# The output projection of a hybrid decoder layer: 648 tokens as block products in two passes over K, the other 384 tokens last

## The chip, the cores and the metric

The kernel runs on one core of a Trainium2 chip. The metric is the device time of one execution in microseconds (us), as the median of several runs. The core's engines work side by side: TensorE multiplies matrices (PE in the profile; PEld are its weight loads), VectorE (DVE) and ScalarE (ACT) do element-wise work, GpSimd (POOL) and SyncE (SP) mostly issue transfers between the core's memory and the chip's DRAM. ACT and POOL issue transfers too. Matmul results land in PSUM, and DVE or ACT must read them out before the bank is used again.

## The reference

One layer for a prompt of 1024 tokens and 8 sample tokens, 1032 tokens in all, in float32. Two branches, a retention and a diagonal state space model (S5), are gated and merged, and the merged rows go through one last projection and a norm:

```
merged = sigmoid(ga) * (ya @ w_pa) + sigmoid(gb) * (yb @ w_pb)     # 1032 x 2048
out = merged @ w_out                                              # w_out: 2048 x 2048
y = x + out * rsqrt(mean(out * out, -1) + EPS) * g_post
```

Only this projection and its norm are changed.

## The kernel before

**Precision.** Each float32 operand is split into a high part (what the matmul's input type holds, made by an ACT copy) and a low part (the rest, made by a DVE subtraction). A product is three matmuls into the same PSUM bank: high by high, high by low, low by high. So every weight tile of 128x512 costs ACT one cast (`whi`) and DVE one subtraction (`wlo`) before TensorE can use it. There are three buffers for each of the two.

**Block products.** All projections ahead of the last one are done by steps (`steps`, line 814). A step makes a 2x2 block of the result with seven products in place of eight, in the manner of Strassen: two output tiles of 128 features (`21` is the second) by two halves of the 1032 tokens, 516 tokens each, with the K dimension (the one that is summed over) also cut in two. The right sides of the seven products are sums and differences of blocks (`FORMS`: u1, t2, v1, t3, t1, t4, v2), made once per projection; the left sides are sums of weight tiles (`s1` to `s4`), made on DVE in each step by `prep`, two products ahead of their use. One product (`product`) is 4 k tiles x 3 matmuls x 2 halves of 258 columns, 24 matmuls. The evacuation after each product (`evac_p`) combines it with the products before it, on DVE, or copies it, on ACT. Products 2, 3, 5 and 6 of a step add into a PSUM tile that an earlier product of the step began, so that TensorE must wait there until the earlier one has been read: a product n+2 cannot start before the evacuation of n.

**The forms of a projection** are staged by `transition`: 28 tiles are loaded through eight buffers (`stg`, issued on POOL's queue) and split, two per product at its height, while the projection before still runs. The program orders work by product number: `at(g, f)` puts f behind product g, `slot()` lets one generator of background work do one piece after each product, and what is issued in order on an engine's queue also runs in order.

**Merge (w_pb, steps SB to SB+7).** `gated` multiplies by the gate. From the third step on, before adds the other branch with a DVE addition from a preloaded tile (`pp`), and writes the merged rows to DRAM (`mg_d`). TensorE's last product of it is followed by the output projection.

**Output projection, before**, is not in block products. (1) `out_rows`: the last 392 tokens stand on the columns; for each of 16 output tiles, 16 k tiles x 3 matmuls of 392 columns (lines 210 to 212, called by `linear`), 768 matmuls. The squares for the norm are made on ACT and added on POOL; the rows are finished in the background. (2) `out_tokens(0, 3, ...)`: the first 640 tokens in chunks of 128 stand as the stationary side, the weights move: 4 groups of 512 features x 16 k tiles x 3 chunks x 3 matmuls of 512 columns (line 1692), 576 matmuls. (3) `out_tokens(3, 2, True)`: the same for the last two chunks, 384 matmuls. In (2) and (3) one weight tile is split anew per k tile and group. In the last group of (3) each chunk is finished as soon as its last matmul is done: square and sum on ACT, product with g_post on DVE, a power on POOL, then four DVE instructions of 512 columns (line 1642), each with its store.

Of the kernel before, what the change touches and what calls it, by code (L numbers as in the profile page):

```python
# [18 lines left out]
D = 2048  # L19
# [8 lines left out]
TA = 640  # L28
SW = TOK - TA
THIRDS = [(0, 384), (384, 768), (768, TOK), (TA, TOK)]  # L30
# [48 lines left out]
def emit(ctx, tc, I, O):  # L79
# [65 lines left out]
    yb_d = dram("yb_d", [8, 128, TOK])  # L145
    mg_d = dram("mg_d", [16, 128, TOK])
# [667 lines left out]
    steps = [(kh, p) for kh in range(2) for p in range(NP)] + [(kh, p) for kh, n in (("glu", 4), ("pa", 8), ("pb", 8)) for p in range(n)]  # L814
    lim = [7 * len(steps)]
    qtile = {}

    def qslot(kh, n, i):
        j = (2 * n + i // 2 + {0: 0, 1: -2, "glu": -4, "pa": -6, "pb": -8}[kh]) % 16
# [7 lines left out]
    def stage(pool, kh, n, i, eng=P):  # L827
        r = stq[kh, n, i] = pool.tile([128, HT], F32, name="stg")
        if kh in (0, 1):
# [13 lines left out]
    def fetch(s):  # L843
# [3 lines left out]
        wd, m, q = (w_in, pairs[p][1], 2 * kh) if kh in (0, 1) else (I["w_" + kh], 2 * p, 0)  # L847
# [33 lines left out]
    def product(g):  # L881
# [7 lines left out]
        for i in range(4):  # L889
            xh, xl = qslot(kh, n, i)  # L890
            for a, b in ((wh, xh), (wh, xl), (wl, xh)):
                for j in range(2):
                    anchor["p"] = T.matmul(ps[:, j, 0:258], a[:, i, :], b[:, 258 * j:258 * j + 258],  # L893
                                           start=first and i == 0 and a is wh and b is xh,
                                           stop=n in (2, 5, 6) and i == 3 and a is wl, skip_group_check=True).ins
        return ps[:, :, 0:258]
# [499 lines left out]
    last_t = {}  # L1396

    def load_z(s, name):
# [4 lines left out]
        if kind == "pb" and p > 1 and (p < 7 or c):  # L1403
            zq[name, "p"] = ppp.tile([128, HT], F32, name="pp")
            A.dma_start(zq[name, "p"], pap_d[2 * p + r, :, HT * c:HT * c + HT])

    def gated(g, name, t, ps=None):
# [19 lines left out]
        elif (name, "p") in zq:  # L1427
            add(t, t, zq.pop((name, "p")), V)
            if c and p > 5:
                last_t[m] = t  # L1430
            P.dma_start(mg_d[m, :, cols], t)
        else:
            P.dma_start(t, pap_d[m, :, cols], accum_op=ALU.add)
            at(g + LAG, lambda: P.dma_start(mg_d[m, :, cols], t))
# [28 lines left out]
    mg, mgr = [None] * KD, {}  # L1463

    def mg_open(m):
        a = act.tile([128, 2, TOK], F32R, name=f"a{(6 + m) % 16}")
        mg[m] = a[:, 0, :], a[:, 1, :]

    def mg_load(m):
        mgr[m] = mgp.tile([128, SW], F32, name="mga")  # L1470
        A.dma_start(mgr[m], mg_d[m, :, TA:TOK])

    def mg_split(m, src=None):
        mg_open(m)
        split((mg[m][0][:, TA:TOK], mg[m][1][:, TA:TOK]), mgr.pop(m) if src is None else src)

    SE = len(steps) - 1
# [41 lines left out]
    for g in sorted(due):  # L1519
        late_work(g)  # L1520
# [273 lines left out]
```

## Time and profile before

| | |
|---|---|
| median of 3 runs (lowest to highest) | 2599.7 us (2599.66 to 2600.05) |
| profiled execution: its time | 2599.76 us |
| profiled execution: span of the trace | 2598.0 us |
| TensorE busy, of the span | 2579.8 us (99%) |
| DVE, ACT, POOL busy | 1900.0 (73%), 968.1 (37%), 686.9 us (26%) |
| mean granted TensorE clock | 0.999 |
| first matmul of the output projection | 2221.76 us |
| its part (2) begins, last matmul begins | 2360.53, 2587.58 us |

The span runs from the first to the last instruction; the execution's own time is 1.8 us longer. A row of a timeline shows start, duration, engine, line, operation, the tile written and the tiles read, and the form; in brackets the idle time of the engine before it and what ended that. Matmuls overlap, so that the pace of a row of matmuls is read from their starts, not from their durations.

### The profile page before, as it was taken

What the parts mean: (1) busy time and instruction counts of PE and PEld (TensorE: products, weight loads), DVE (VectorE), ACT (ScalarE), POOL (GpSimd) and SP (SyncE); (2) the same over time, 40 slices, a digit from 0 to 9 for tenths busy, and PEclk for the clock granted to TensorE, in tenths of its full rate; (3) what the DMA queues carried; (4) which work ended last, traced back from release to release, by engine and by line L of the source; (5) the groups of instructions that cost most, each with busy time, mean ns of one, the idle gap of its engine ahead of it and who ended that gap; (6) DMA issues with size and microseconds to landing.
All of it is one profiled execution on the core that took longest, in us unless ns stands there. A gap on an engine that the chain in (4) does not pass through costs nothing.

```text
span 2598.0 us, 51727 instructions
## 1 busy us (share of the span) xinstructions
PE 2579.8 (99%) x19748; PEld 2517.0 (97%) x19748; DVE 1900.0 (73%) x3949; ACT 968.1 (37%) x1707; POOL 686.9 (26%) x1140
## 2 busy tenths in 40 slices
PE   9999999999999999999999999999999999999998
PEld 8999999999999999999999999999999999998876
DVE  7655988898898877558976766677787878545555
ACT  6113233233233334343334444435542422443344
POOL 0103312222222222332334434334222221111011
PEclk9999999999999999999999999999999999999999
DMA  5886534434444437887788888888787786755667
GB/s 193 263 261 218 152 116 121 138 117 127 134 119 134 127 117 251 205 214 190 199 207 230 226 223 218 212 217 257 254 288 256 235 225 211 232 165 180 184 199 234
DMA packets 234072, 509.79 MB, mean 196 GB/s; under 512 B 32753, under 2 KB 55233, under 8 KB 233697
## 3 DMA queue, kind: packets, MB, share of 16 engines
q0 software_dynamic: 92496, 271.74, 37.4%
q1 hardware_dynamic: 103072, 177.46, 22.6%
q10 hardware_dynamic: 38256, 57.30, 7.3%
q8 instruction: 155, 2.54, 0.4%
q14 instruction: 93, 0.75, 0.1%
HBM read 343.74 MB, written 162.64 MB: 195 GB/s over the span
## 4 chain that ended last, share of the span: by engine, by line
PE 96%; DVE 2%; issue 1%; DMA 1%; ACT 1%; DVEq 0%; POOLq 0%; POOL 0%; ACTq 0%; SPq 0%
PE acc L893 68%; PE acc L1692 9%; PE mm L212 2%; PE mm L210 2%; PE mm L211 2%; PE acc L210 2%; PE acc L211 2%; PE acc L212 2%; PE misc L635 1%; PE misc L713 1%; PE misc L712 1%; PE misc L1097 1%; PE misc L1107 1%; PE misc L1076 1%; PE misc L663 1%
## 5 line engine op out<-in xcount | busy, mean ns | idle before, releaser
L893 PE MATMUL acc<-a,whi 128*128 128x258 f32 x10080 | 1635.2, 284 | 1.0 <-ACT whi L874 0.6
L893 PEld LDWEIGHTS acc<-a,whi 128*128 128x128 f32 x10080 | 1387.9, 190 | 5.5 <-issue 2.4
L893 PE MATMUL acc<-a,wlo 128*128 128x258 f32 x5040 | 1014.3, 282 | 0.0
L893 PEld LDWEIGHTS acc<-a,wlo 128*128 128x128 f32 x5040 | 779.5, 189 | 0.0
L84 DVE TENSOR_TENSOR wlo<-wraw,whi 128x512 fp32r<-128x512 f32 x496 | 340.1, 686 | 259.6 <-ACT whi L203 141.2
L874 ACT CAST whi<-wraw 128x512 fp32r<-128x512 f32 x360 | 223.5, 621 | 638.2 <-PE acc L893 473.3
L874 ACT CAST whi<-wr 128x512 fp32r<-128x512 f32 x270 | 167.4, 620 | 531.3 <-PE acc L893 459.8
L84 DVE TENSOR_TENSOR wlo<-wr,whi 128x512 fp32r<-128x512 f32 x270 | 184.6, 684 | 42.3 <-ACT whi L874 41.2
L1692 PE MATMUL acc<-whi,a 128*128 128x512 f32 x640 | 201.9, 396 | 0.0
L203 ACT CAST whi<-wraw 128x512 fp32r<-128x512 f32 x136 | 84.1, 620 | 203.8 <-PE acc L1692 69.0
L210 PE MATMUL mm<-a,whi 128*128 128x384 f32 (+1 forms) x448 | 145.0, 325 | 4.9 <-ACT whi L203 4.8
L1692 PEld LDWEIGHTS acc<-whi,a 128*128 128x128 f32 x640 | 120.2, 188 | 30.2 <-DVE z L84 2.1
L211 PE MATMUL mm<-a,whi 128*128 128x384 f32 (+1 forms) x448 | 145.1, 324 | 0.2 <-DVE a L364 0.2
L212 PE MATMUL mm<-a,wlo 128*128 128x384 f32 (+1 forms) x448 | 144.7, 323 | 0.1
L1692 PE MATMUL acc<-wlo,a 128*128 128x512 f32 x320 | 127.0, 397 | 0.0
L84 DVE TENSOR_TENSOR wraw<-wr 128x512 f32<-128x512 f32 x180 | 123.4, 685 | 2.5
L84 DVE TENSOR_TENSOR wlo<-wx,whi 128x512 fp32r<-128x512 f32 x78 | 53.8, 691 | 71.9 <-ACT whi L203 71.7
L84 DVE TENSOR_TENSOR u<-acc,p 128x516 f32<-128x516 f32 x90 | 62.2, 691 | 57.8 <-PE acc L893 55.8
L84 DVE TENSOR_TENSOR u<-acc,u 128x516 f32<-128x516 f32 x90 | 62.3, 693 | 54.6 <-PE acc L893 53.8
L84 DVE TENSOR_TENSOR p<-acc,p 128x516 f32<-128x516 f32 x90 | 62.3, 692 | 50.3 <-PE acc L893 50.2
L84 DVE TENSOR_TENSOR a<-stg,a 128x516 fp32r<-128x516 f32 x140 | 91.7, 689 | 7.0 <-DMA stg<-fm_d 4.0
L203 ACT CAST whi<-wx 128x512 fp32r<-128x512 f32 x78 | 48.4, 620 | 123.6 <-PE acc L1692 45.0
(373 smaller groups left out, 3496.2 us busy)
## 6 DMA issues: line engine op xcount, KB each, us to landing
wr<-in_w_in SPq DMA_DIRECT2D x280, 256.0 KB
pt_d<-u POOLq DMA_DIRECT2D x70, 258.0 KB, 3.3
u<-pt_d POOLq DMA_DIRECT2D x70, 258.0 KB, 5.0
wraw<-in_w_outB SPq DMA_DIRECT2D x65, 256.0 KB
wx<-in_w_outB SPq DMA_DIRECT2D x45, 256.0 KB
stg<-fm_d POOLq DMA_DIRECT2D x44, 258.0 KB, 4.5
wraw<-in_w_out SPq DMA_DIRECT2D x39, 256.0 KB
pt_d<-st POOLq DMA_DIRECT2D x35, 258.0 KB, 3.4
```

What stands on the lines that cost most here:

```text
L84: return (eng or V).tensor_tensor(out, a, b, op)
L203: anchor["a"] = A.copy(hi, raw).ins
L210: T.matmul(ps, wh[:, i, :], xh[:, t0:t1], start=first, stop=False)
L211: T.matmul(ps, wh[:, i, :], xl[:, t0:t1], start=False, stop=False)
L212: anchor["p"] = T.matmul(ps, wl[:, i, :], xh[:, t0:t1], start=False, stop=last).ins
L635: T.matmul(ps[0:16, g * 128:(g + 1) * 128], B1[:, g, :], W3[:, g, 0:8, :], start=True, stop=True)
L663: T.matmul(ps[:, q * 144:(q + 1) * 144], W1[:, g, :], U[:, g, :], start=True, stop=True)
L712: T.matmul(o, Tm[:, g, :], U[:, g, 0:136], start=True, stop=False)
L713: T.matmul(o, W3[:, g, 1:9, :], X[:, g, 0:136], start=False, stop=True)
L874: anchor["a"] = A.copy(hi, f).ins
L893: anchor["p"] = T.matmul(ps[:, j, 0:258], a[:, i, :], b[:, 258 * j:258 * j + 258], start=first and i == 0 and a is wh and b is xh, stop=n ...
L1692: anchor["p"] = T.matmul(ps[c], a, b, start=k == 0 and a is xh and b is wh, stop=k == KD - 1 and a is xl).ins
```

## The change

The boundary between the two ways of working moves from token 640 to token 384 (`TA`), and the columns' share (648 tokens, `SW`; half of it is `HO`, 324) is done in block products like the projections ahead of it:

- Two new kinds of step, `o0` and `o1`, eight steps each: K is taken in two passes of 1024, each of them 8 pairs of output tiles x 7 products x 4 k tiles x 3 matmuls of 324 columns, 1344 matmuls together. They stand right behind the steps of w_pb and use the same `prep`, `fetch` and `product`.
- Their right sides: `forms_o` makes the four sums per pair of k tiles on DVE from `mg_d` and stores them (`fo_d`); `transition` stages and splits 28 tiles of 324 columns for each pass. For `o0` this happens in the last steps of w_pb and the first of `o0`, for `o1` in the last two of `o0` and the first of `o1`. `forms_o(1)` runs in the first two steps of `o0`.
- `evac_o`: pass `o0` writes its results to DRAM (`pt_d`), pass `o1` adds these to its own by an accumulating transfer that POOL issues.
- The merge's addition in DVE (`pp`) is gone; all of w_pb's results get the other branch by an accumulating transfer.
- `rows_out` is the norm and the finish of the 648 tokens: squares on ACT, each put in the order six products behind its accumulating transfer, sums on DVE (32 quarters of an output pair), then 32 x two DVE instructions and a store, in the background of the last chunks.
- The first 384 tokens come last, in one run of three chunks (576 matmuls of 512 columns, line 1736); the chunks of parts (2) and (3) above are no more two runs of three and two. Their merged rows are loaded and split by `split_m` in the last step of `o1` and in the first group. In the last group each chunk is finished with one DVE instruction of 2048 columns, the third chunk with one of 1024 and two of 512.

```diff
-TA = 640
+TA = 384
 SW = TOK - TA
+HO = SW // 2
...
-    steps = [(kh, p) for kh in range(2) for p in range(NP)] + [(kh, p) for kh, n in (("glu", 4), ("pa", 8), ("pb", 8)) for p in range(n)]
+    steps = [(kh, p) for kh in range(2) for p in range(NP)] + [(kh, p) for kh, n in (("glu", 4), ("pa", 8), ("pb", 8), ("o0", 8), ("o1", 8)) for p in range(n)]
...
         for i in range(4):
             xh, xl = qslot(kh, n, i)
             for a, b in ((wh, xh), (wh, xl), (wl, xh)):
-                for j in range(2):
-                    anchor["p"] = T.matmul(ps[:, j, 0:258], a[:, i, :], b[:, 258 * j:258 * j + 258],
+                for o, x in ([(ps[:, 0, 0:HO], b)] if kh in OUTS else [(ps[:, j, 0:258], b[:, 258 * j:258 * j + 258]) for j in range(2)]):
+                    anchor["p"] = T.matmul(o, a[:, i, :], x,
...
-        elif (name, "p") in zq:
-            add(t, t, zq.pop((name, "p")), V)
...
         else:
             P.dma_start(t, pap_d[m, :, cols], accum_op=ALU.add)
             at(g + LAG, lambda: P.dma_start(mg_d[m, :, cols], t))
...
-    for m in (15, 14):
-        mg_split(m, last_t[m][:, TA - HT:HT])
...
+    def forms_o(kh, wait):
+        t, w = {}, {}
+        def ld(i):
+            if i < 2:
+                w[i] = act.tile([128, 2, TOK], F32, name=f"a{(6, 4)[kh] + i}")
+            t[i] = w[i % 2][:, 0, 0:SW], w[i % 2][:, 1, 0:SW]
+            for x, k in zip(t[i], (8 * kh + i, 8 * kh + 4 + i)):
+                P.dma_start(x, mg_d[k, :, TA:TOK])
+        for i in range(4):
+            if i % 2 == 0:
+                if i:
+                    yield
+                ld(i)
+                if i:
+                    yield
+                ld(i + 1)
+                for _ in range(wait):
+                    yield
+            u, v = t.pop(i)
+            u1, u2, v1, v2 = u[:, 0:HO], u[:, HO:SW], v[:, 0:HO], v[:, HO:SW]
+            sub(u1, u1, u2)
+            sub(u2, u2, v2)
+            yield
+            add(v2, v2, u1)
+            sub(v1, v1, v2)
+            P.dma_start(fo_d[kh, 0, i], u)
+            P.dma_start(fo_d[kh, 1, i], v)
...
+    def merged(m):
+        f, b = flat(4 + m // 2, "m", F32R), 2 * TA * (m % 2)
+        return f[:, b:b + TA], f[:, b + TA:b + 2 * TA]
+    def spare(m):
+        b = 4 * HO + TA * (m % 2)
+        return flat(2 + m // 2 % 2, "z")[:, b:b + TA]
+    def load_m(m):
+        P.dma_start(spare(m), mg_d[m, :, 0:TA])
+    def split_m(m):
+        split(merged(m), spare(m))
+        if m + 4 < KD:
+            load_m(m + 4)
...
+    def evac_o(g, ps):
+        s, n = divmod(g, 7)
+        kind, p = steps[s]
+        two_ = kind == "o1"
+        def done(name, t):
+            r, c = AT[name]
+            if not two_:
+                P.dma_start(pt_d[2 * p + r, c, :, 0:HO], t)
+            else:
+                P.dma_start(t, pt_d[2 * p + r, c, :, 0:HO], accum_op=ALU.add)
+                ready[2 * p + r, c] = g + 6, t
...
+        if n == 0:
+            A.copy(tile_("p1"), ps)
+        elif n == 1:
+            sub(tile_("u2"), cur["p1"], ps)
+        elif n == 2:
+            t = zplace(2 * p, 0) if two_ else st_tile()[:, 0:HO]
+            A.copy(t, ps)
+            done("11", t)
...
+    def rows_out():
+        order = [(2 * p + r, c) for p in range(8) for r, c in ((0, 0), (1, 1), (1, 0), (0, 1))]
+        seen = set()
+        for m, c in order:
+            while (m, c) not in ready or ready[m, c][0] > now[0]:
+                yield
+            z, h = ready[m, c][1], ssq[:, HO * c:HO * c + HO]
+            if c not in seen:
+                seen.add(c)
+                A.activation(h, z, AF.Square)
+            else:
+                q = st_tile()[:, 0:HO]
+                A.activation(q, z, AF.Square)
+                if now[0] < lim[0]:
+                    yield
+                add(h, h, q)
+            yield
+        def xr(i):
+            return flat(0, "x")[:, HO * (i % 6):HO * (i % 6) + HO]
+        order.sort()
+        def ld(i):
+            if i < 32:
+                m, c = order[i]
+                A.dma_start(xr(i), I["xT"][m, :, TA + HO * c:TA + HO * c + HO])
+        for i in range(5):
+            ld(i)
+        yield from rms_bcast(ssq, ssq, const)
+        yield
+        yield
+        for i, (m, c) in enumerate(order):
+            z = ready[m, c][1]
+            V.scalar_tensor_tensor(z, z, gpost[:, m:m + 1], ssq[:, HO * c:HO * c + HO], ALU.mult, ALU.mult)
+            add(z, z, xr(i))
+            P.dma_start(O["yA"][m, :, HO * c:HO * c + HO], z)
+            ld(i + 5)
+            yield
+        for c in (1, 2):
+            P.dma_start(x_of(c), I["xB"][c])
...
+        if s == SB + 4:
+            bg.append(forms_o(0, 2))
...
+        if s == SO:
...
+            bg.append(forms_o(1, 3))
...
+            bg.append(rows_out())
...
+            transition(g, SB + 6, "o0")
+            transition(g, SP - 2, "o1")
...
-    out_rows()
-    stage_pool(512, 2)
-    out_tokens(0, 3, False)
-    out_tokens(3, 2, True)
-    drain()
...
+        if g == 3:
+            V.scalar_tensor_tensor(r1, s4[:, 3:4], 1.0 / D, r1, ALU.mult, ALU.add)
+            P.tensor_tensor(r3, r1, r2, ALU.pow)
+            for i, (a, b) in enumerate(((0, D),) if c < 2 else ((0, 1024), (1024, 1536), (1536, D))):
+                z = flat(12 + c, "zc")[:, a:b]
+                V.scalar_tensor_tensor(z, z, r3, x_of(c)[:, a:b], ALU.mult, ALU.add)
+                (A if i % 2 else nc.sync).dma_start(O["yB"][c, :, a:b], z)
...
+    rest = deque(range(6, KD))
+    for g in range(4):
+        both_ = banks_of["pst"].tile([128, 2, 512], F32, name="acc")
+        ps = [both_[:, 0, :], both_[:, 1, :], mmbank()]
+        e = 11 if g == 3 else 13
+        todo_ = [[(k, c) for c in range(3)] for k in range(e)] + [[(k, c) for k in range(e, KD)] for c in range(3)]
+        for st in todo_:
+            for k, c in st:
+                while order_w and order_w[0] <= (g, k + 1):
+                    next_w()
+                wh, wl = wb[g, k]
+                xh, xl = (a[:, 128 * c:128 * c + 128] for a in merged(k))
+                for a, b in ((xh, wh), (xh, wl), (xl, wh)):
+                    anchor["p"] = T.matmul(ps[c], a, b, start=k == 0 and a is xh and b is wh, stop=k == KD - 1 and a is xl).ins
+                if k == KD - 1:
+                    evac_c(g, c, ps[c])
+            now[0] += 1
+            if rest:
+                with ExitStack() as after:
+                    for ins in anchor.values():
+                        after.enter_context(tc.issue_after(ins))
+                    split_m(rest.popleft())
+            slot()
+        if g == 2:
+            drain()```

`flat(j, ...)` is the memory of the 16 big tiles `a0` to `a15`, `zplace` a place for a quarter of the result, and `next_w` splits one weight tile for the chunks.

How this moves the instructions is shown at three places. First TensorE's own order where the merge ends (names with `a_` are right sides, `whi` and `wlo` the weights' two parts, `acc` is PSUM). Before:

```order
L893 MATMUL acc<-a_26492,whi 128x258 x4
L893 MATMUL acc<-a_26492,wlo 128x258 x2
L210 MATMUL acc<-a_28058,whi 128x392
L211 MATMUL acc<-a_28058,whi 128x392
L212 MATMUL acc<-a_28058,wlo 128x392
```

With the change:

```order
L919 MATMUL acc<-a_26493,whi 128x258 x4
L919 MATMUL acc<-a_26493,wlo 128x258 x2
L919 MATMUL acc<-a_27986,whi 128x324 x2
L919 MATMUL acc<-a_27986,wlo 128x324
L919 MATMUL acc<-a_28062,whi 128x324 x2
L919 MATMUL acc<-a_28062,wlo 128x324
```

In place of the 768 matmuls of 392 columns stand 1344 of 324 columns, three per k tile as before.

Second, DVE's order at the same place. Before, in the last step of the merge (`a_` with `mga` are low parts of merged rows, `u_`, `p_` and `st` are evacuations and gates):

```order
L84 TENSOR_TENSOR a_28226<-mga,a_28226 128x392
L84 TENSOR_TENSOR u_28261<-acc,p_28131 128x516
L84 TENSOR_TENSOR wlo<-wr,whi 128x512
L84 TENSOR_TENSOR a_28265<-mga,a_28265 128x392
L84 TENSOR_TENSOR a_28268<-mga,a_28268 128x392
L84 TENSOR_TENSOR wlo<-wraw,whi 128x512
L84 TENSOR_TENSOR u_28261<-u_28261,acc 128x516
L84 TENSOR_TENSOR u_28261<-u_28261,zz 128x516
L84 TENSOR_TENSOR a_28310<-mga,a_28310 128x392
L84 TENSOR_TENSOR u_28261<-u_28261,pp 128x516
```

With the change, in the first step of `o0`, from the evacuation of product 3 on (`a_28444` and `a_28447` are the sums of `forms_o(1)`, `a_28557<-stg` splits of staged tiles, `wraw` sums of weights):

```order
L85 TENSOR_TENSOR u_28526<-acc,p_28433 128x324
L85 TENSOR_TENSOR a_28444<-a_28444 128x324
L85 TENSOR_TENSOR wraw<-wr,wraw 128x512
L85 TENSOR_TENSOR u_28526<-u_28526,acc 128x324
L85 TENSOR_TENSOR wlo<-wraw,whi 128x512
L85 TENSOR_TENSOR a_28557<-stg,a_28557 128x324 x2
L85 TENSOR_TENSOR wlo<-wr,whi 128x512
L85 TENSOR_TENSOR p_28433<-acc,p_28433 128x324
L85 TENSOR_TENSOR a_28447<-a_28447 128x324
L85 TENSOR_TENSOR wraw<-wraw,wr 128x512
L85 TENSOR_TENSOR u_28477<-acc,u_28477 128x324
L85 TENSOR_TENSOR wlo<-wraw,whi 128x512
```

Splits, sums of the forms, sums of weights and evacuations stand between one another in one queue, from evacuation 1 of that step to evacuation 1 of the next 31 instructions: 11 of 512 columns and 20 of 324. In a later step of `o0` it is 16 (11 and 5); around the start of `o1` it is 27 (10 and 17), then 26 (13 and 13).

Third, DVE's end of the program. Before, for the last two chunks:

```order
L84 TENSOR_TENSOR z_31577<-acc,z_28405 128x512
L1637 SCALAR_TENSOR_TENSOR small<-small 128x1
L1642 SCALAR_TENSOR_TENSOR z_30971<-z_30971,small 128x512
L1642 SCALAR_TENSOR_TENSOR z_31175<-z_31175,small 128x512
L1642 SCALAR_TENSOR_TENSOR z_31380<-z_31380,small 128x512
L1642 SCALAR_TENSOR_TENSOR z_31577<-z_31577,small 128x512
```

With the change, for the last three:

```order
L1719 SCALAR_TENSOR_TENSOR a_31357<-a_31357,small,a_31037 128x2048
L85 TENSOR_TENSOR a_31374<-acc,a_31035 128x512
L1715 SCALAR_TENSOR_TENSOR small<-small 128x1
L1719 SCALAR_TENSOR_TENSOR a_31374<-a_31374,small,a_31939 128x2048
L85 TENSOR_TENSOR a_31391<-acc,a_31035 128x512
L1715 SCALAR_TENSOR_TENSOR small<-small 128x1
L1719 SCALAR_TENSOR_TENSOR a_31391<-a_31391,small,a_31941 128x1024
L1719 SCALAR_TENSOR_TENSOR a_31391<-a_31391,small,a_31941 128x512 x2
```

A chunk's product with g_post now stands behind one instruction of 2048 columns of the chunk before, where it stood behind four of 512.

321 lines of the change are left out of this document (115 added, 206 removed).

## The prediction

> **What bounds the kernel now.** First the page: the busy times, the chain of waits that ended last, the costliest groups.
>
> ```profile
> span 2598.0 us, 51727 instructions
> ...
> PE 2579.8 (99%) x19748; PEld 2517.0 (97%) x19748; DVE 1900.0 (73%) x3949; ACT 968.1 (37%) x1707; POOL 686.9 (26%) x1140
> ...
> PE 96%; DVE 2%; issue 1%; DMA 1%; ACT 1%; DVEq 0%; POOLq 0%; POOL 0%; ACTq 0%; SPq 0%
> ...
> L1692 PE MATMUL acc<-whi,a 128*128 128x512 f32 x640 | 201.9, 396 | 0.0
> ```
>
> TensorE is 96% of the chain. A change pays here by what it takes from TensorE's stream, and costs by every gap that it makes there. What the stage is worth is read from the chain from 2200 us on, and from where its matmuls start and end.
>
> ```profile
> 2199.95 13.34 PE acc L893 x111
> ...
> 2222.96 0.45 PE acc L212
> ...
> 2360.70 6.27 PE acc L1692 x27
> 2366.97 0.69 PE misc L267 x8
> ...
> 2369.95 0.44 PE misc L289 x4
> ...
> 2370.62 0.73 PE misc L289 x4
> 2371.35 129.17 PE acc L1692 x552
> ...
> 2547.23 38.68 PE acc L1692 x164
> ```
> ```profile
> 2221.52 0.41 PE L893 MATMUL acc<-a,wlo 128*128 128x258 f32 x2
> 2221.76 0.34 PE L210 MATMUL acc<-a,whi 128*128 128x392 f32 x1
> ...
> 2222.96 0.45 PE L212 MATMUL acc<-a,wlo 128*128 128x392 f32 x1 [0.69 <-DVE wlo L84]
> ```
> ```profile
> 2587.35 0.39 PE L1692 MATMUL acc<-wlo,a 128*128 128x512 f32 x1
> ...
> 2587.58 0.40 PE L1692 MATMUL acc<-whi,a 128*128 128x512 f32 x1
> ```
>
> The output projection holds TensorE from 2221.76 to 2587.98 us, 366.2 us; in that time 1.9 us went to the norm's small matmuls (0.69 + 0.44 + 0.73) and 0.69 us to a wait for DVE where the merge ends. Nothing else in the row is a gap worth a term. Behind the last matmul 10.0 us remain to the end of the span.
>
> **Term 1: TensorE's own work.** What a matmul of 324 columns costs no row shows; rows on both sides of it do. In the first phase the same triple (high, low, weights' low) runs with 384 and with 264 columns, one weight load per matmul, as the change has it:
>
> ```profile
> 60.14 0.33 PE L210 MATMUL mm<-a,whi 128*128 128x384 f32 x1
> ...
> 63.45 0.34 PE L211 MATMUL mm<-a,whi 128*128 128x384 f32 x1
> ...
> 63.80 0.29 PE L210 MATMUL mm<-a,whi 128*128 128x264 f32 x1
> ...
> 65.03 0.28 PE L211 MATMUL mm<-a,whi 128*128 128x264 f32 x1
> ```
> ```profile
> L212 PEld LDWEIGHTS acc<-a,wlo x256: 186/187/192, 2223.0 to 2360.2; 128*128 128x128 f32 x128
> L212 PE MATMUL acc<-a,wlo x256: 336/340/446, 2223.0 to 2360.4; 128*128 128x392 f32 x128
> ```
>
> From start to start: 384 columns 3.31 us / 19 = 174 ns, 264 columns 1.23 / 10 = 123 ns; 324 lies midway, 149 ns. The 392 columns of the stage itself: (2360.4 - 2223.0) / (255 x 3) = 180 ns. The 258 columns of the steps, by the 24 matmuls of a product (2.88 us in a step of 20.18, below): 120 ns. A line between these two gives 149 ns too. I take 149; the ends are 148 and 151 (258's cost per column). The two passes: 1344 x 0.149 = 200.3 us (199 to 203). The three chunks keep the pace of 129.17 / 552 = 0.234: 576 x 0.234 = 134.8. The norm's small matmuls go from four pieces of 128 tokens to six: 1.9 x 6/4 = 2.8. Together 337.9, against 366.2: **-28.3 us**.
>
> **Term 2: DVE at the seams.** A product takes TensorE 24 x 0.120 = 2.88 us in the merge, 12 x 0.149 = 1.79 us in the passes, a step of seven 12.5 us; but the weights' work per product stays as it was. So I read DVE where it is densest now, the staging of w_pb's forms, with one step as a window:
>
> ```profile
> 2040.14:2060.32 20.18, 20.18 (x171) 20.18 (x170) 19.58 (x32) 12.29 (x22) 8.53 (x17) 1.00 0.89 295
> ```
> ```profile
> 2041.68 0.69 DVE L84 TENSOR_TENSOR u<-u,zz 128x516 f32<-128x516 f32 x1
> 2042.57 1.30 DVE L84 TENSOR_TENSOR a<-stg,a 128x516 fp32r<-128x516 f32 x2 [0.20 <-ACT a L257]
> 2043.79 0.68 DVE L84 TENSOR_TENSOR wlo<-wraw,whi 128x512 fp32r<-128x512 f32 x1
> ```
> ```profile
> L84 DVE TENSOR_TENSOR a<-z,a 128x640 fp32r<-128x640 f32 x16 | 13.2, 825 | 3.2 <-ACT a L257 3.2
> ...
> L84 DVE TENSOR_TENSOR z<-z,sz 128x392 f32<-128x392 f32 x16 | 9.0, 564 | 0.4
> ```
>
> DVE is 97% busy there with 32 instructions, and TensorE (the second number) doesn't stop. Two in a row take 1.30, one 0.69: the next begins 0.61 us after the first, 0.08 before it ends. From 640 to 392 columns a duration falls by 0.261 us, 1.05 ns per column; 324 columns then last 0.564 - 68 x 0.00105 = 0.49 and pace at 0.41 (estimates). A quiet step of the passes has 11 DVE instructions of 512 columns (seven low parts, four weight sums) and 5 evacuations: 11 x 0.61 + 5 x 0.41 = 8.8 of 12.5 us. In the second pass four sums of squares more: 10.4. Both fit. At the seams they don't. First step of the first pass: 11 and 20 (the last splits, and half of the second pass's sums): 6.7 + 8.2 = 14.9, 2.4 over. The second step, 12 and 11, is 11.8. The start of the second pass: 10 and 17 = 13.1, then 13 and 13 = 13.3: 0.6 and 0.8 over. Sum **+3.8 us** of stalls, late being a low part (`wlo`) or an evacuation that TensorE's next product but one waits for. The lower end is 0: evacuations may lag by most of a product, 1.8 us, before TensorE notices, and the small overruns may drown in that. The upper end prices each at its full duration (0.69 and 0.49): 17.4, 13.7, 15.2 and 15.4, together 11.7 over. I take the pace, as the window above shows DVE keeping it, and give no credit for the lag, since a DVE that waits for ACT's cast in between loses some.
>
> **Term 3: the end.** The last chunk's path is now: matmul, square, product with g_post, power, finish, store. Before:
>
> ```profile
> 2588.02 0.58 ACT L1629 ACTIVATE misc<-acc 128x512 f32<-128x512 f32 x1 [1.40 <-PE acc L1692]
> 2588.09 2.74 DVE L1642 SCALAR_TENSOR_TENSOR z<-z,small 128x512 f32<-128x512 f32 x4 [0.68 <-POOL small L1638]
> ...
> 2590.75 0.68 DVE L84 TENSOR_TENSOR z<-acc,z 128x512 f32<-128x512 f32 x1
> 2591.35 0.15 DVE L1637 SCALAR_TENSOR_TENSOR small<-small 128x1 f32<-128x1 f32 x1
> ...
> 2592.16 2.74 DVE L1642 SCALAR_TENSOR_TENSOR z<-z,small 128x512 f32<-128x512 f32 x4 [0.66 <-POOL small L1638]
> ```
>
> The last product waited for the four instructions of the chunk before (to 2590.8); from there 0.6, 0.8 for the power, 2.74 for the finish, 3.1 for the store. With the change the chunks' last matmuls lie 15 x 0.234 = 3.5 us apart. One finish of 2048 columns, at 1.05 ns per column above 0.685 for 512, is 2.3 us. The first chunk, done 7.0 us before the last matmul ends (E), is finished at E - 2.4 (0.8 square, 0.6 product, 0.8 power, 2.3); the second's product then goes at E - 2.4, its finish ends at E + 1.3; the third's product runs to E + 1.9, power to 2.7, three parts of 1.2 + 0.7 + 0.7 to 5.3, store 3.1: E + 8.4, against 10.0. **-1.6 us**, other end 0 (the longer stores get in one another's way).
>
> **At nothing:** the merge's addition on DVE is gone and its accumulating transfer new, both under TensorE's products of 2.88 us. The 384 tokens' splits (32 instructions) and the 32 rows' finish (64 DVE instructions of about 0.45 us, 29 us) lie under 134.8 us of chunks, where DVE's other work is 64 low parts (39 us); uncovered, that last would be 29 us.
>
> **Sum** against the profiled execution: 2599.76 - 28.3 + 3.8 - 1.6 = 2573.7 us; the median of the runs is 2599.7, so **2573.6**.
>
> **The rivals.** *R1: DVE bounds both passes through.* DVE stands in order, and each low part needs ACT's cast first:
>
> ```profile
> 2574.62 0.69 DVE L84 TENSOR_TENSOR wlo<-wx,whi 128x512 fp32r<-128x512 f32 x1 [0.70 <-ACT whi L203]
> ```
>
> If every one of seven low parts per step costs such a wait w, a step is 8.8 + 7w: with 0.70, 13.7 us, 1.2 over 12.5, 19 us in 16 steps: 2593. From w = 0.76 on (16 x (7w - 3.7) = 26) the kernel is slower than before; with w = 0.9, 42 us, 2615. For it: the margin per step is only 3.7 us. Against: in that row ACT's cast itself waited for TensorE to free a buffer, and in the full window above DVE found other work. *R2: the accumulating transfers, the other side.* In the second pass ACT squares a quarter six products, 10.7 us, behind its evacuation; ACT's next casts queue behind that square, and TensorE behind them.
>
> ```profile
> p<-pap_d POOLq DMA_DIRECT2D x3, 258.0 KB, 5.8
> ```
>
> Such a transfer took 5.8 us from issue to landing, with 0.9 us on POOL's queue ahead:
>
> ```profile
> L1433 POOL DMA_DIRECT2D u<-pap_d x4: 865/920/1238, 2077.6 to 2107.9; - x4
> ```
>
> At L us in place of 10.7, 56 products lose (L - 10.7) / 6 each; from L = 13.5 on it is slower; at 15, 40 us, 2614. Against: 6.7 leaves 4 us. *R3: it doesn't do what it says, since a matmul can't follow faster than its weight load.* The load rows last 187 ns: 1344 x (0.187 - 0.149) = 51 us, 2625. Against: the 264-column rows run at 123 ns with a load each. [...]
>
> **How the numbers follow.** My forecast has 80 in 100 (own range 2569 to 2583: terms 2 and 3 at their ends), R1 12 (9 faster, 1 same, 2 slower), R2 5 (2, 1, 2), R3 3. A change under 0.2%, 5 us, can't be told from none. So faster 0.91, same 0.02, slower 0.07. The range 2568.5 to 2588 leaves out R3, most of R2 and the far half of R1.
>
> **What would show it.** Right: 1344 matmuls of 324 columns at 148 to 151 ns from start to start; TensorE's gaps for DVE or ACT of 2 to 6 us in the first step of each pass, next to none elsewhere; the last matmul some 24 us earlier; the tail about 8.5 us. Wrong: gaps in every step with DVE over 95% busy (R1), ACT's squares waiting for transfers (R2), 324 columns at 180 ns or more (R3), or the rows' finish reaching into the last group of chunks.

## The result, and the profile after

The changed kernel took **2617.9 us** (median of 4 runs, 2614.9 to 2621.2) against 2599.7 us (4 runs, 2599.5 to 2600.1): a ratio of 1.007, 95% interval 1.0053 to 1.0088. It is 18 us slower, where 26 us faster was forecast. The profiled execution took 2619.0 us, its span 2617.1.

The page of the changed kernel first: busy times and the chain of waits.

```profile
PE 2565.9 (98%) x19948; PEld 2518.0 (96%) x19948; DVE 1983.2 (76%) x4159; ACT 971.5 (37%) x1747; POOL 784.4 (30%) x1300
...
PE 81%; issue 6%; DMA 6%; DVE 3%; POOL 3%; ACT 1%; POOLq 0%; DVEq 0%; ACTq 0%; SPq 0%
...
PE acc L919 63%; PE acc L1736 5%; PE mm L214 2%; PE mm L212 2%; PE mm L213 2%; DMA u<-pap_d 1%; DMA fo_d<-a 1%; DVE a L85 1%; DMA a<-mg_d 1%; DMA st<-pap_d 1%; PE misc L637 1%; PE misc L715 1%; PE misc L714 1%; DVE wlo L85 1%; PE misc L1133
```

TensorE is busy 13.9 us less than before (2579.8), and the span is 19.1 us longer. Its share of the chain fell from 96 to 81%; DMA, POOL and "issue" took it, and among the lines named in it stand `u<-pap_d` and `st<-pap_d`, the accumulating transfers of the merge. Those stand before the part that the change was written for. The stretch 2080 to 2221.5 us is the merge (w_pb), as a window: before, then changed, then the rest of the changed merge, up to its first product of 324 columns at 2249.70.

```profile
2080.00:2221.50 141.50, 141.50 (x1181) 141.50 (x1180) 108.00 (x169) 40.05 (x70) 22.45 (x37) 1.00 0.76 228
```
```profile
2080.00:2221.50 141.50, 130.63 (x1044) 129.50 (x1043) 84.84 (x139) 31.18 (x54) 45.27 (x68) 0.96 0.84 224
...
2221.50:2249.70 28.20, 19.26 (x144) 18.88 (x144) 16.97 (x32) 8.85 (x19) 13.84 (x22) 0.88 0.86 228
```

Columns: length, then busy time of PE, PEld, DVE, ACT and POOL, the granted clock, the DMA engines' share, GB/s. Before, TensorE has no gap; now it is idle for 10.9 + 8.9 us, and its granted clock is 0.96 and 0.88. No other engine is near full. The same matmuls that were done at 2221.8 are done at 2249.7.

Where the time went, by stage, from the first and last matmul of each (before's stages are in the prediction; all traces agree to within 1 us up to 2080 us):

| us | predicted | changed | gap |
|---|---|---|---|
| merge, from 2080 | 141.8 | 169.7 | +27.9 |
| two passes (1344 matmuls of 324) | 204.1 | 216.5 | +12.4 |
| chunks and the norm's small matmuls | 137.6 | 140.3 | +2.7 |
| tail | 8.4 | 10.7 | +2.3 |

Together 45.3 us, the whole distance from 2573.7 to 2619.0. TensorE's waits in the merge (instructions in order of time; in brackets the idle time before each and what ended it):

```profile
2151.06 1.23 PE L919 MATMUL acc<-a,whi 128*128 128x258 f32 x4 [3.69 <-ACT p L1457]
...
2242.33 1.20 PE L919 MATMUL acc<-a,whi 128*128 128x258 f32 x4 [7.50 <-DVE u L85]
```

`p` and `u` are evacuations of a product, and they are late in two ways. ACT is late with `p` because the buffer that it writes isn't free: its last contents are not yet stored (`mg_d<-p`). DVE is late with `u` because, in order, a split of a staged tile (`a<-stg`) stands ahead of it, ACT's half of that split stands still, and the tile's load has not landed:

```profile
2150.42 0.59 ACT L1457 COPY p<-acc 128x516 f32<-128x516 f32 x1 [5.52 <-DMA mg_d<-p]
...
2240.59 0.46 ACT L259 CAST a<-stg 128x324 fp32r<-128x324 f32 x1 [5.66 <-DMA stg<-mg_d]
...
2241.08 0.50 DVE L85 TENSOR_TENSOR a<-stg,a 128x324 fp32r<-128x324 f32 x1 [5.62 <-ACT a L259]
```

The second way cost more: the next longest gap too, 5.0 us at 2187.74, stands behind a DVE sum that waited 4.1 us for its load (`a<-mg_d`). Both the stores and these loads are issued by POOL:

```profile
2126.11 0.93 POOL L1450 DMA_DIRECT2D st<-pap_d  x1
2132.86 0.56 POOL L1451 DMA_DIRECT2D mg_d<-st  x1 [5.82 <-DMA st<-pap_d]
2133.40 0.90 POOL L1450 DMA_DIRECT2D u<-pap_d  x1
2140.16 0.56 POOL L1451 DMA_DIRECT2D mg_d<-u  x1 [5.85 <-DMA u<-pap_d]
...
2150.86 1.07 POOL L1489 DMA_DIRECT2D a<-mg_d  x2 [2.35 <-DMA mg_d<-p]
2151.92 0.93 POOL L1450 DMA_DIRECT2D st<-pap_d  x1
```

L1450 starts the accumulating transfer of a quarter, L1451 stores the sum. The store stands right behind its own transfer or one transfer further on (the delay of four products in the code is not seen in POOL's order), POOL works in order, and so it stands still until the transfer has landed, for up to 5.8 us and 3.0 on average; everything behind waits with it, the next accumulating transfer first, then the loads for the output projection (L1489, `stg`). Over 2080 to 2250 us these waits are, by the waits view of POOL:

```profile
POOL mg_d L1451 <- DMA u<-pap_d: 33.0, 14, 5.8
POOL mg_d L1451 <- DMA st<-pap_d: 24.9, 6, 5.8
POOL mg_d L1451 <- DMA p<-pap_d: 24.1, 7, 5.4
```

These are 82 us of 170 (columns: total, times, longest). From one step's `st` (2126.11) to the next (2151.92) POOL needs 25.8 us, where TensorE's step takes 20.18.

### The profile page after: what moved, and what is told of

Same layout as the page of the kernel before. It is cut to its first block, busy times and chain, and to the rows that moved or that the text cites. A ratio compares the mean times of both kernels' runs of the same rounds, so it can differ in the third digit from the quotient of the medians.

```text
span 2617.1 us, 52507 instructions
## 1 busy us (share of the span) xinstructions
PE 2565.9 (98%) x19948; PEld 2518.0 (96%) x19948; DVE 1983.2 (76%) x4159; ACT 971.5 (37%) x1747; POOL 784.4 (30%) x1300
## 4 chain that ended last, share of the span: by engine, by line
PE 81%; issue 6%; DMA 6%; DVE 3%; POOL 3%; ACT 1%; POOLq 0%; DVEq 0%; ACTq 0%; SPq 0%
PE acc L919 63%; PE acc L1736 5%; PE mm L214 2%; PE mm L212 2%; PE mm L213 2%; DMA u<-pap_d 1%; DMA fo_d<-a 1%; DVE a L85 1%; DMA a<-mg_d 1%; DMA st<-pap_d 1%; PE misc L637 1%; PE misc L715 1%; PE misc L714 1%; DVE wlo L85 1%; PE misc L1133 1%
## 5 line engine op out<-in xcount | busy, mean ns | idle before, releaser
L919 PE MATMUL acc<-a,whi 128*128 128x258 f32 (+1 forms) x10976 | 1844.0, 287 | 30.9 <-DVE u L85 22.3
L919 PEld LDWEIGHTS acc<-a,whi 128*128 128x128 f32 x10976 | 1545.2, 190 | 39.3 <-ACT whi L900 12.2
L919 PE MATMUL acc<-a,wlo 128*128 128x258 f32 (+1 forms) x5488 | 1156.8, 285 | 0.5 <-DVE wlo L85 0.5
L919 PEld LDWEIGHTS acc<-a,wlo 128*128 128x128 f32 x5488 | 866.9, 190 | 1.0 <-DVE wlo L85 1.0
L900 ACT CAST whi<-wraw 128x512 fp32r<-128x512 f32 x424 | 263.2, 621 | 690.0 <-PE acc L919 512.4
L85 DVE TENSOR_TENSOR wlo<-wraw,whi 128x512 fp32r<-128x512 f32 x456 | 312.7, 686 | 173.3 <-ACT whi L900 114.2
L900 ACT CAST whi<-wr 128x512 fp32r<-128x512 f32 x318 | 197.3, 621 | 567.3 <-PE acc L919 511.1
L85 DVE TENSOR_TENSOR wlo<-wr,whi 128x512 fp32r<-128x512 f32 x380 | 260.7, 686 | 72.7 <-ACT whi L900 41.7
L212 PE MATMUL mm<-a,whi 128*128 128x384 f32 (+1 forms) x448 | 145.1, 326 | 5.6 <-ACT whi L205 5.6
L85 DVE TENSOR_TENSOR wraw<-wr 128x512 f32<-128x512 f32 x212 | 145.5, 686 | 2.7
L213 PE MATMUL mm<-a,whi 128*128 128x384 f32 (+1 forms) x448 | 145.2, 324 | 0.1
L214 PE MATMUL mm<-a,wlo 128*128 128x384 f32 (+1 forms) x448 | 144.8, 323 | 0.1
L85 DVE TENSOR_TENSOR a<-stg,a 128x516 fp32r<-128x516 f32 (+1 forms) x196 | 118.0, 632 | 32.2 <-ACT a L259 27.9
L259 ACT CAST a<-stg 128x516 fp32r<-128x516 f32 (+1 forms) x196 | 104.8, 574 | 48.5 <-DMA stg<-mg_d 17.8
L1736 PE MATMUL acc<-whi,a 128*128 128x512 f32 x372 | 117.8, 395 | 1.9 <-ACT whi L205 1.9
L85 DVE TENSOR_TENSOR u<-acc,p 128x516 f32<-128x516 f32 (+1 forms) x106 | 70.1, 661 | 57.3 <-PE acc L919 56.7
L85 DVE TENSOR_TENSOR u<-acc,u 128x516 f32<-128x516 f32 (+1 forms) x100 | 67.3, 673 | 58.7 <-PE acc L919 57.7
L85 DVE TENSOR_TENSOR p<-acc,p 128x516 f32<-128x516 f32 (+1 forms) x100 | 67.2, 672 | 53.3 <-PE acc L919 53.2
L85 DVE TENSOR_TENSOR u<-p,acc 128x516 f32<-128x516 f32 (+1 forms) x106 | 69.7, 657 | 32.5 <-PE acc L919 12.9
L212 PEld LDWEIGHTS mm<-a,whi 128*128 128x128 f32 x448 | 84.5, 189 | 5.8 <-ACT whi L205 5.6
```

The costliest lines, as they stand in the source:

```text
L85: return (eng or V).tensor_tensor(out, a, b, op)
L212: T.matmul(ps, wh[:, i, :], xh[:, t0:t1], start=first, stop=False)
L213: T.matmul(ps, wh[:, i, :], xl[:, t0:t1], start=False, stop=False)
L214: anchor["p"] = T.matmul(ps, wl[:, i, :], xh[:, t0:t1], start=False, stop=last).ins
L259: A.copy(dst[0], src)
L900: anchor["a"] = A.copy(hi, f).ins
```

## Experiments

Two rival readings of the merge were set against that one (theory Q, POOL's queue): F, that the new sums and splits for the output projection overload DVE; M, that the DMA engines (0.84 busy) are the limit.

**The merge's addition back on DVE.**

```diff
+        if kind == "pb" and p > 1:
+            zq[name, "p"] = ppp.tile([128, HT], F32, name="pp")
+            A.dma_start(zq[name, "p"], pap_d[2 * p + r, :, HT * c:HT * c + HT])
...
+        elif (name, "p") in zq:
+            add(t, t, zq.pop((name, "p")), V)
+            P.dma_start(mg_d[m, :, cols], t)
...
```

Further lines open and close the buffers `pp`.

> The changed kernel, with the merge's addition back on DVE from the third step of w_pb on (the earlier product loaded on ACT's queue into three buffers, added, stored once from POOL), as in the kernel before; all else as changed. Theory Q (POOL's queue): in the changed merge each store stands on POOL right behind its accumulating transfer and waits 4 to 6 us for it to land, so that a step holds POOL 22 to 26 us against TensorE's 20.18, and buffers come free late. Then the merge (2080 us to the first product of 324 columns, 171.5 us in the changed kernel) comes back to 141 to 147 us and the whole time to 2577 to 2588 us. Rival F (the forms' new sums, staging and splits overload DVE in the last steps of the merge): DVE gets 24 more additions, so no gain, 2616 to 2625. Rival M (the DMA engines, busy 0.84 there in place of 0.76, are the limit): the same bytes are still moved, 2608 to 2618.

Measured: 2585.0 us (2582.6 to 2587.8), ratio to the kernel before 0.9939 (0.9922 to 0.9956). The window of the merge:

```profile
2080.00:2221.50 141.50, 141.50 (x1181) 141.50 (x1180) 117.44 (x195) 41.03 (x74) 42.48 (x75) 1.00 0.89 282
```

TensorE is full again, with DVE busier (117 us, not 85) and the DMA engines too (0.89). TensorE reaches its first product of 324 columns 142.4 us after 2080. F and M fall; Q's numbers hold, for the merge (141 to 147) and for the whole. One edit turns 18 us slower into 15 us faster.

**The same transfers in another order.** Each store is put behind the accumulating transfers of the next two quarters:

```diff
+    landing = deque()
...
-            P.dma_start(t, pap_d[m, :, cols], accum_op=ALU.add)
-            at(g + LAG, lambda: P.dma_start(mg_d[m, :, cols], t))
+            landing.append((mg_d[m, :, cols], t))
+            with tc.issue_after(P.dma_start(t, pap_d[m, :, cols], accum_op=ALU.add).ins):
+                if len(landing) > 2:
+                    P.dma_start(*landing.popleft())
...
```

`issue_after` holds the store behind the transfer just issued; further lines store the last quarters when the merge ends.

> The changed kernel with its accumulating transfers all kept, and only the place of the merged quarter's store changed: it is issued on POOL behind the accumulating transfers of the next two quarters, not right behind its own. Same transfers, same bytes, same DVE work. Theory Q: the wait in front of each store falls from 4 to 6 us to under 1 us for most, a step's POOL work falls under 20.18 us, TensorE's gaps of the merge go: 2577 to 2592 us. Rivals F and M: nothing that they blame has changed, 2613 to 2621.

Measured: 2592.8 us (2590.4 to 2594.9), ratio 0.9971 (0.9959 to 0.9983), just past Q's upper bound. By the groups of instructions in 2080 to 2250 us (count, then busy, mean ns, and behind the second bar the idle time before them), the stores' waits are gone, 0.9 + 0.0 + 0.6 us in place of 82:

```profile
L1455 POOL DMA_DIRECT2D mg_d<-u x15 | 13.7, 911 | 0.9 <-issue 0.9
...
L1455 POOL DMA_DIRECT2D mg_d<-st x8 | 7.7, 963 | 0.0
...
L1455 POOL DMA_DIRECT2D mg_d<-p x7 | 5.5, 793 | 0.6 <-DMA mg_d<-u 0.4 <-issue 0.2
```

```profile
2080.00:2221.50 141.50, 139.76 (x1160) 139.20 (x1159) 101.58 (x169) 39.45 (x72) 60.48 (x94) 1.00 0.96 269
```

With the DMA engines at 0.96 in the merge (the window above) TensorE lost 1.7 of 141.5 us, so bytes weren't the limit. This is the cleanest of the tests, since it removes no work at all. POOL's waiting at the stores fell from 82 us to 1.5, and 3.0 more at the last two stores of the merge. What stays, some 8 us against the DVE version, lies largely in the first step of the first pass (gaps of 6.7 us, against 3.3 in the DVE version): a stored quarter is now two quarters later, so are the loads that read it, and ACT, waiting for one, holds TensorE's weights.

```profile
2239.47 0.46 ACT L259 CAST a<-stg 128x324 fp32r<-128x324 f32 x1 [3.41 <-DMA stg<-mg_d]
```

**The stores on SP's queue**, in place of POOL's:

```diff
-            at(g + LAG, lambda: P.dma_start(mg_d[m, :, cols], t))
+            at(g + LAG, lambda: nc.sync.dma_start(mg_d[m, :, cols], t))
```

> The changed kernel with the merged quarters' stores issued on SP's queue (which issues the weights' loads) instead of POOL's. Theory Q: POOL no longer stands behind a landing, the merge comes back to 142 to 150 us; SP now stands behind it, 28 stores of up to 6 us, and its weight loads come later, which the one step of prefetch should mostly cover: 2578 to 2600. Rivals F and M: 2613 to 2621.

Measured: 2586.5 us (2583.7 to 2589.0), ratio 0.9948 (0.9933 to 0.9962), as Q expects. SP now stands still for the landings (2080 to 2250 us), and TensorE doesn't notice:

```profile
SPq L1451 <- DMA u<-pap_d: 40.7, 15, 7.8
SPq L1451 <- DMA p<-pap_d: 39.8, 8, 5.9
SPq L1451 <- DMA st<-pap_d: 37.6, 7, 8.8
```

118 us of waiting, more than POOL had, and free (the merge takes 141.9 us): what stands behind it on SP are loads of weights that nobody needs for a step. Here the wait had no price of its own; what was queued behind it had.

**The accumulating transfers alone.** The kernel before, with them in all steps of w_pb but the last (which stays as it was), and none of the new output projection:

```diff
-        if kind == "pb" and p > 1 and (p < 7 or c):
+        if kind == "pb" and p > 6 and c:
...
+            if c and p > 5:
+                last_t[m] = t
```

> The kernel before, with the accumulating transfer and its store in all steps of w_pb but the last (in place of the first two only): the changed kernel's merge without the forms for the output projection. Theory Q: its first two steps already hold POOL some 24 us each, so POOL falls behind by 4 us per step, some 25 us by the seventh; TensorE can lend about 14 us (a quarter's buffer is wanted again 9 products later), so gaps begin in the last two or three steps and the output stage's loads come late: 2605 to 2635 us in place of 2599.7. Rival F: 2599 to 2601. Rival M: 2599 to 2603, the DMA engines stay under 0.85.

Measured: 2607.8 us (2607.6 to 2610.1), ratio 1.0032 (1.002 to 1.0044): 8 us slower. Within Q's range, but not as Q said. There is no gap in the merge. An early step of POOL's took 23.8 us, a late one 20.5:

```profile
2092.71 0.90 POOL L1435 DMA_DIRECT2D st<-pap_d  x1
...
2116.53 0.93 POOL L1435 DMA_DIRECT2D st<-pap_d  x1
...
2178.69 0.93 POOL L1435 DMA_DIRECT2D st<-pap_d  x1
...
2199.14 0.93 POOL L1435 DMA_DIRECT2D st<-pap_d  x1
```

By the last of these rows POOL is 8 us behind TensorE's pace (the first such row is at 2070.16, and six steps take 121.1 us). Over the last three steps shown it nearly kept pace, because the transfers landed sooner: the store of `st` began 7.6 us after its transfer in the step from 2092.71, 4.9 us after it in the step from 2178.69. Why they landed sooner stays open, and the step behind these rows took 23.0 us again. The 8 us are paid at the seam, where the merge ends: there ACT waits for a quarter to land, and the weights' casts behind it are late (TensorE busy 24.2 of 28.5 us, clock 0.88):

```profile
2221.40 0.52 ACT L257 CAST a<-u 128x392 fp32r<-128x392 f32 x1 [4.93 <-DMA u<-pap_d]
```
```profile
2221.50:2250.00 28.50, 24.18 (x115) 23.02 (x114) 12.52 (x21) 11.13 (x22) 6.26 (x9) 0.88 0.77 248
```

So the transfers alone fill POOL to the brim (20.3 to 23.8 us a step), the new loads alone fit (first experiment), and only the two on one queue make the merge's 28 us. My extrapolation of 4 us lost in every step was wrong.

**What is left: three edits for three gaps.** The first experiment's trace still had a gap of 3.2 us in the chunks, two in the first step of the first pass, one at the start of the second, and a tail of 11.0 us.

```profile
2234.79 0.54 PE L919 MATMUL acc<-a,whi 128*128 128x324 f32 x2 [1.52 <-DVE u L85]
2240.69 1.09 PE L919 MATMUL acc<-a,whi 128*128 128x324 f32 x4 [1.77 <-ACT whi L900]
...
2341.20 0.56 PE L919 MATMUL acc<-a,whi 128*128 128x324 f32 x2 [1.22 <-ACT whi L900]
...
2445.34 0.50 PE L1746 MATMUL acc<-whi,a 128*128 128x512 f32 x1 [3.23 <-ACT whi L205]
```

The edits: two loads of 1 MB (the row of g_post, not shown, and the first x) written behind the 384 tokens' splits, not ahead; the last group's chunks held in order; the sums for the second pass two steps later.

```diff
         if s == SO:
             zstack.close()
-            bg.append(forms_o(1, 3))
+        if s == SO + 2:
+            bg.append(forms_o(1, 3))
...
-    P.dma_start(x_of(0), I["xB"][0])
...
                     split_m(rest.popleft())
+                    if not rest:
+                        P.dma_start(x_of(0), I["xB"][0])
...
+                        if g == 3 and k == e and c and a is xh and b is wh:
+                            after.enter_context(tc.issue_after(anchor["p"]))
...
```

On the DVE version:

> The addition back on DVE (as in the first experiment), and three small edits on what its trace still shows, each to be read in its own window: (a) the row of g_post and the first chunk's x (1 MB each) are loaded only when the last of the 384 tokens' splits has been issued, not ahead of them; (b) in the last group of chunks the second and third chunk's matmuls are held behind the one before (they were interleaved, so that the last two chunks end 1.9 us apart, not 3.5); (c) the sums for the second pass start two steps of the first pass later. My theory of each: (a) the gap of 3.2 us 14 us into the chunks goes, with the 3.4 us of half clock behind it, -5 us; (b) the tail falls from 11.1 us to 8.5 to 9, -2; (c) TensorE's gaps in the first step of the first pass (1.5 and 1.8 us, and 3.4 us of half clock behind them) shrink to under 1.5 us, -3. Sum: 2585 - 10 = 2575 us (2571 to 2579). Rival: each wait has another right behind it (the g_post row late for the first product, weights late for three k in a row, the second pass's forms late): 2581 to 2590.

On the SP version:

> The same three edits on the kernel whose merged stores go by SP and whose accumulating transfers stay. By my theory 2586.5 - 10 = 2576 us (2572 to 2581), the merge 1 to 2 us above that of the DVE version where SP's weights come late; by the rival 2582 to 2592.

Measured: 2580.8 us (2579.9 to 2582.0), ratio 0.9927 (0.9913 to 0.994); and 2582.6 us (2581.6 to 2584.3), ratio 0.9933 (0.9921 to 0.9946). 4 of the expected 10 us came in either version, both times lay past the upper end of my range, and the edits fared differently. The later sums (c) did what was expected in the DVE version: no gap over 0.4 us in the first step, and the passes last 204.2 us (209.2 without them, in the slowest of the first experiment's runs); in the SP version one of 2.0 us stayed, where ACT, and DVE behind it, waits for a quarter that the merge stores late:

```profile
2231.02 0.46 ACT L259 CAST a<-stg 128x324 fp32r<-128x324 f32 x1 [2.10 <-DMA stg<-mg_d]
```

The order of the loads (a) helped only in part. Written later in the program, the first of the two large loads still stands ahead of several blocks' loads in POOL's order and started as early as before, 0.8 us ahead of the chunks; the other started 6.3 us behind the chunks' start, not 2.7. The gap was still 1.9 us. In the DVE version:

```profile
2439.00 0.50 PE L1748 MATMUL acc<-whi,a 128*128 128x512 f32 x1 [1.93 <-ACT whi L205]
```
```profile
2425.72 0.55 POOL L1759 DMA_DIRECT2D a<-in_xB  x1
```
```profile
2437.92 0.51 ACT L259 CAST a<-a 128x384 fp32r<-128x384 f32 x1 [5.18 <-DMA a<-mg_d]
```

It is the same pattern on another engine: ACT's split of a block waits 5.2 us for its load, and the cast of the next weights, ready long since, stands behind it. The ordered chunks (b) brought the tail to 9.5 us and made a new wait, the rival of this run: the second chunk's first matmul waits 1.5 us for DVE's product of the first, since their banks belong to one tile.

**Splits three rows later, and the chunks in the order first, third, second:**

```diff
-            for i, (a, b) in enumerate(((0, D),) if c < 2 else ((0, 1024), (1024, 1536), (1536, D))):
+            for i, (a, b) in enumerate(((0, D),) if c != 1 else ((0, 1024), (1024, 1536), (1536, D))):
...
-    rest = deque(range(6, KD))
+    rest, NG = deque(range(6, KD)), now[0]
...
-        todo_ = [[(k, c) for c in range(3)] for k in range(e)] + [[(k, c) for k in range(e, KD)] for c in range(3)]
+        todo_ = [[(k, c) for c in range(3)] for k in range(e)] + [[(k, c) for k in range(e, KD)] for c in ((0, 2, 1) if g == 3 else range(3))]
...
-            if rest:
+            if rest and now[0] - NG > 3:
...
```

`NG` is the count of products at which the chunks begin; the finish in three parts goes to the second chunk, which now ends last.

> The kernel of the fifth experiment with two edits on what its trace still shows: the last ten splits of the 384 tokens are issued three products' rows (3 x 9 matmuls, 6.3 us) later, so that ACT, which does them in order between its casts of the weights, comes to each only when its load has landed; and the last group ends in the order first, third, second chunk, since the second chunk's bank waits for DVE's product of the first. My theory: the gap of 2.2 us, 12 us into the chunks, goes (-2.2), and so does the 1.5 us wait for DVE in the last group (-1.5), the tail staying at 9 to 9.5 us: 2580.8 - 3.7 = 2577 us (2575 to 2579). Rival: the later splits are late for their matmuls, or the loads behind them (four places in a ring) are: 2580 to 2588.

Measured: **2576.6 us** (2576.1 to 2577.1), ratio 0.9908 (0.9892 to 0.9925), 24 us faster than the kernel before. Both gaps are gone. Its passes, chunks and tail as windows:

```profile
2222.65:2427.21 204.56, 202.08 (x1347) 199.86 (x1346) 182.28 (x340) 105.30 (x213) 74.89 (x122) 1.00 0.71 195
2427.21:2565.11 137.90, 137.46 (x602) 109.82 (x600) 93.40 (x182) 52.11 (x101) 27.07 (x47) 1.00 0.71 236
2565.11:2574.80 9.69, 0.00 (x0) 0.00 (x0) 4.57 (x6) 0.69 (x2) 0.55 (x1) 0.62 0.65 258
```

204.6, 137.9 and 9.7 us stand against the 204.1, 137.6 and 8.4 predicted for the changed kernel. That the passes agree says little of the prediction's second term: the sums that it put into the first step have been moved out of it here.

## Why the prediction was wrong

**The step that failed** is "At nothing: the merge's addition on DVE is gone and its accumulating transfer new, both under TensorE's products of 2.88 us". What the transfer costs was looked up (0.9 us on POOL, 5.8 us to landing), and it was put under TensorE's work; the store behind it, which makes POOL wait for that landing, was not counted, nor the queue as a whole. Four quarters a step, with a landing in front of each store and the new loads between, are more than 20.18 us. It cost 27.9 us in the merge and, with POOL late into the first pass, part of the 12.4 us there: undoing it alone gave 33 us back.

The trace before shows it, in the two steps that worked in this way already. One step of POOL there:

```profile
2093.20 0.90 POOL L1433 DMA_DIRECT2D st<-pap_d  x1
2100.21 0.56 POOL L1434 DMA_DIRECT2D mg_d<-st  x1 [6.10 <-DMA st<-pap_d]
2100.75 0.91 POOL L1433 DMA_DIRECT2D u<-pap_d  x1
2106.82 0.56 POOL L1434 DMA_DIRECT2D mg_d<-u  x1 [5.16 <-DMA u<-pap_d]
...
2117.09 0.57 POOL L1434 DMA_DIRECT2D mg_d<-u  x1 [1.63 <-DMA u<-pap_d]
```

24.5 us from the first row to the end of the last, against 20.18, on an engine that the page gives as 26% busy: the waits aren't counted. Read with POOL's new loads in the same steps, these rows would have made a rival.

**Term 1** (-28.3) held. 324 columns follow each other at 149.8 ns and 512 at 233.2, from the chain of the changed kernel (start, length, count), where 149 and 234 were predicted:

```profile
2291.22 59.17 PE acc L919 x395
...
2494.76 109.84 PE acc L1736 x471
```

**Term 2** (+3.8) named the right places. With the merge repaired (the gaps quoted from the first experiment), the first step lost 1.5 + 1.8 us and the start of the second pass 1.8 with its small gaps, 5.1 of the 5.4 us that TensorE was idle in the passes; 3.4 us of half clock (clock 0.68 and 0.75 from 2241 to 2244 and from 2244 to 2247 us) cost 1.7 more. Moving the second pass's sums two steps on took the first step's gaps away in the DVE version. That fits the term: in the first experiment DVE worked 15.3 us from evacuation 1 of that step to evacuation 1 of the next, where 14.9 was estimated and TensorE has 12.5. But the edit moved the sums' loads and stores on POOL as well, and a split had waited 2.7 us for its load in that step (DVE stood idle for 0.9 of them), so that the shares of the two causes are not told apart. The SP version shows the second by itself: the merge's last quarters landing late, which the term left out. At the start of the second pass the term's mechanism does not hold. DVE stood idle for 1.4 us there, behind a split whose load was late; that the 1.8 us lost come near the 1.4 predicted (0.6 + 0.8) is luck:

```profile
2338.38 0.91 ACT L259 CAST a<-stg 128x324 fp32r<-128x324 f32 x2 [2.41 <-DMA stg<-mg_d]
```

**Term 3** (-1.6) had the wrong sign: the tail is 10.7 us, 0.7 more than before. It was worked out for chunks that end 3.5 us apart. In the changed program the third chunk's first matmuls stand between the second's, so that the last two end 1.9 us apart, and the third's product waits behind the second's whole finish:

```profile
2604.62 0.58 ACT L1707 ACTIVATE misc<-acc 128x512 f32<-128x512 f32 x1 [4.55 <-PE acc L1736]
...
2606.53 0.58 ACT L1707 ACTIVATE misc<-acc 128x512 f32<-128x512 f32 x1 [1.22 <-PE acc L1736]
2606.77 2.35 DVE L1719 SCALAR_TENSOR_TENSOR a<-a,small,a 128x2048 f32<-128x2048 f32 x1 [0.67 <-POOL small L1716]
...
2609.04 0.68 DVE L85 TENSOR_TENSOR a<-acc,a 128x512 f32<-128x512 f32 x1
```

Even at 3.5 us apart, in the last experiment, the tail was 9.7 us, 1.3 over the estimate. The last finish ended 5.2 us behind the last matmul, as worked out (5.3); the store behind it took 4.5 us, not 3.1.

**"At nothing", the chunks:** the splits of the 384 tokens were put under 134.8 us by DVE's sum of work. What they cost was not work but order: ACT, waiting for a load, held the weights' casts, 2.2 us in the changed kernel, 3.5 in the first experiment, nothing once issued later.

**The rivals.** R1 (DVE bounds both passes) fell: the quiet steps have no gaps (none over 0.2 us from 2292 to 2372 us in the changed kernel). R3 (324 columns at 187 ns, its 3 in 100 an estimate that no run bears out) fell with 149.8: at this size the weight load sets no bound that shows. R2 came near: it took the accumulating transfers as the danger, but in the second pass, by ACT's squares; there the last experiment has no gap over 1.2 us. No rival looked at the merge.

## What to carry over

An accumulating transfer followed by a store of the same tile kept its queue here until the transfer had landed (3.0 us on average on POOL in the changed kernel, up to 5.8; up to 8.8 on SP); count a queue's time per step with these waits in it, and read it off the timeline, since the busy share leaves them out (POOL was busy for 59 of the 169.7 us of the changed merge, next to 82 us of these waits). Whether the wait cost was decided by what was queued behind it: on POOL, with the new loads behind it, 28 us in the merge, on SP none there. Where a stage's working set moves to another queue, look at the stage ahead of it too, for it shares the queue.

## What the runs showed of the hardware

In these traces TensorE's granted clock went from 1.0 to 0.5 after some gaps, or within them, and this added to what a gap cost. Behind the first long gap of the changed kernel (columns as above, the clock third from the end):

```profile
2154.00:2159.00 5.00, 5.00 (x33) 5.00 (x32) 2.60 (x5) 0.62 (x1) 1.27 (x2) 0.70 0.65 166
2159.00:2164.00 5.00, 5.00 (x43) 5.00 (x43) 4.08 (x8) 1.24 (x2) 0.18 (x1) 1.00 0.91 231
```

From 2154 to 2159 TensorE is busy throughout and does 33 matmuls in place of 43. By the clock's records in the trace the changed kernel was at half speed for 23.9 us before its end, in five pieces of 3.4 or 6.8 us. For 4.3 us of these TensorE was idle (3.4 of them in the gap of 7.5 us), so that it worked 19.6 us at half speed, a loss of some 10 us which is part of the 45. The kernel before had none. Half clock came also where the longest single gap was 1.8 us (2241 to 2244 us of the first experiment, clock 0.68), and stayed away after 1.9 and 0.2 us (the row at 2439.00 above, clock 1.00 around it). The same gap of 1.93 us for the same cast stands in the SP version of that experiment, at 2441.87, and there the matmuls of 512 columns followed each other at 0.43 us from 2443.19 to 2445.32, and at 0.23 from 2445.59 on: the length of a gap does not decide by itself. What does, and whether it is behind the 6 us over which the changed kernel's runs spread (the kernel before: 0.5), no run here was made to show.
